# Neighbourhood attention on TensorE: low products with 66 stationary columns, placed between a step's transposes

## The chip, the cores and the metric

The kernel runs on one core of a Trainium2 chip. The metric is the device time of one execution in microseconds (us); of several runs the median is taken. The engines that matter here are TensorE (PE, with its weight loads as PEld), VectorE (DVE), ScalarE (ACT) and GpSimd (POOL). SyncE (SP) issues most of the DMA transfers. A matrix product on PE has a stationary operand, loaded first (here up to 128 columns, each giving one row of the output), and a moving operand that is streamed through it (here 128 to 512 columns).

## The reference

The reference is an encoder of two layers over 1024 tokens of width 1024. Layer 0 mixes tokens with mixer A, layer 1 with mixer B, and behind each mixer comes a gated embedding; everything is float32. The change touches mixer A alone. Tokens lie on a grid 64 wide, and each query attends to a window of 8 rows by 16 columns around it, with a bias by head and offset. Cut to what matters:

```python
proj = h @ w_in
q, k, v, gate = jnp.split(proj, 4, axis=-1)        # 16 heads of 64
...
def row_block(args):
    ...
    sc = jnp.einsum('bhqd,bhqnd->bhqn', qb, kg) * scale
    sc = sc + bb[None]
    pr = jax.nn.softmax(sc, axis=-1)
    return jnp.einsum('bhqn,bhqnd->bhqd', pr, vg)
...
return (o * jax.nn.silu(gate)) @ w_out
```

## The kernel before, in words

**Precision.** Products run on PE in fp32r, a rounded float32. To keep float32's accuracy each operand is split into a high part and a low part (what the rounding left), and three of the four products are added up: high by high, high by low, low by high. In names `h` and `l` at the end are the two parts: `HTh`/`HTl` the normalised activations, `wh`/`wl` a weight tile, `PTh`/`PTl` the attention weights transposed.

**Tiling of mixer A.** The 1024 tokens are 8 tiles of 128. A tile's window reaches into its own tile and its two neighbours, so an inner tile has three pieces of 128 keys and an outer one has two. The main loop runs over 16 heads h and 8 tiles j; a pair (h, j) is a step. It occupies the stretch from 64 to 520 us of the profiled execution. Each step issues a piece of a pipeline:

- `f_S` (line 741): scores of the step three ahead, two products `s<-KA,QS` and `s<-KB,QS`; DVE then adds the bias table (line 760).
- `f_E` (765): ACT's exponential of the step two ahead, in `sp`.
- `f_T` (770): this step's weights are transposed on PE, two transposes `t<-ident,sp` (776). Two tiles are enough for three pieces, since the two outer pieces of an inner tile use complementary rows and share one tile. ACT copies them to `PTh` (781), DVE takes the rest to `PTl` (782), and for inner tiles POOL parts the shared piece into two by masks (`apart`, 786), first of `PTh`, then of `PTl`. These two land in the key tiles j−1 and j+1.
- `f_AV` (793): the products with v of the step three behind, for the key tile kb: `o<-PTh,V`, then `o<-PTl,V` (the "high" and the "low" product). `V` has 128 stationary columns: 64 of v's high part and 64 of its low part, so an output `o` has 128 rows, and `head_end` adds the upper 64 to the lower ones later. A key tile serves the queries of up to three tiles, so the moving operand is 256 or 384 columns wide; for kb 3 and 4 it is split in two (256 and 128 columns), as the queries 0 to 3 and 4 to 7 have outputs of their own. The products of kb need the masks of tiles kb−1 and kb+1, so the last `PTh` that they wait for is that of tile kb+1, transposed two steps ahead of them. After kb 4 and kb 7 half a head is complete and `head_end` (482) is called.

**What sets the order.** Everything is written out by hand in program order, one queue per engine. `mix` (366) interleaves a list `att` of the steps' pieces with a list of dense blocks (projections of q, k and the gate for later heads: six products of 512 columns to a block) by costs; after each piece or block a counter ticks. `CA` (31) holds the costs: head, f_T, f_E, f_S, f_AV = 1.0, .5, 1.25, 1.0, .75. What `head_end` leaves for later (`post`) is due so many ticks after it: among it `rows` (496), which transposes the reciprocal row sums on DVE (`r8T`, 498), stores them to DRAM by four DMAs (`rD`, 501) and reads them back, spread over 64 partitions, by two (`rb`, 503). Then comes `fin` (563), POOL's products `Y*G` (574) and `Y*rb` (575). All these DMAs stand in SP's queue, and there the weight loads of `Weights.stage` (`wstage`, 211; two stage buffers) stand too. ACT splits a weight tile to `wh` (228) when it has landed, DVE subtracts for `wl` (233). Every fourth head (3, 7, 11) also computes v for the next four heads behind its products.

Of the kernel before, what the change touches and what calls it, by code (L numbers as in the profile page):

```python
# [21 lines left out]
NT = 8  # L22
# [3 lines left out]
NH = 16  # L26
# [4 lines left out]
CA = (1.0, 0.5, 1.25, 1.0, 0.75)  # L31
# [7 lines left out]
FIN = (4, 4)  # L39
# [10 lines left out]
YS = (11, 11)  # L50
YLOAD_A, YLOAD_B = 0, 118
OPEN3 = 5
ULOAD = 5
TAGS_A = [("th", 512, 2), ("tb", 640, 2), None, ("G", 512, 3)]
TAGS_B = [("th", 512, 2)]
# [105 lines left out]
def trunk(ctx, tc, x, wts, rpb, gains, hgains, mask, sides, rope, gain0, out):  # L161
# [118 lines left out]
    def load_y(l, t):  # L280
        for i, (d, src) in enumerate(zip((HTh, HTl), yD[l])):
            k0 = 4 if i and t >= 4 else 0
            (act if t < 4 else sync).dma_start(d[:, t, k0:7].bitcast(F32), src[t, :, k0:7])
# [34 lines left out]
    def mm(ps, a, b, first, last):  # L318
        pe.matmul(ps, a, b, start=first, stop=last, skip_group_check=True)  # L319
# [333 lines left out]
    def mixer_a():  # L653
        jobs = weight_sums()
        with ExitStack() as es:
# [4 lines left out]
            sb = es.enter_context(tc.tile_pool(name="asb", bufs=2))  # L660
            V = one.tile([128, NT, 4, 128], F32R, name="V")
# [9 lines left out]
            gg, ylive = {}, {}  # L671
            QS, KA, KB, TB, RS, SP, OP, UT = {}, {}, {}, {}, {}, {}, {}, {}
            later = Later()

            def v_items(qd, t, thirds=None):
                keys = [("av", qd, 0), ("av", qd, 1)]

                def evac(ps):
                    v = ps.rearrange("p (h d) -> p h d", h=4)
                    act.activation(V[:, t, :, 0:64], v, AF.Copy)  # L680
                    dve.tensor_tensor(V[:, t, :, 64:128], v, V[:, t, :, 0:64], ALU.subtract)
                return [d[0] for d in proj_N(keys, t, 256, valloc, evac, release=keys if t == NT - 1 else (), thirds=thirds)]
# [39 lines left out]
            def load_u(h):  # L722
                UT[h] = sb.tile([128, 16, 24], F32, name="u", bufs=1)
                sync.dma_start(UT[h], U2[h].rearrange("p (r c) -> p r c", r=16))

            def table(h):
                u = UT.pop(h)
                tb = sb.tile([128, 640], F32, name="tb").rearrange("p (k c) -> p k c", k=5)
                for k, c0 in ((0, 0), (1, 0), (2, 8), (3, 16), (4, 16)):
                    pool.tensor_tensor(tb[:, k].rearrange("p (r c) -> p r c", r=16),  # L730
                                       MK[:, k].rearrange("p (r c) -> p r c", r=16),
                                       u[:, :, c0:c0 + 8], ALU.subtract)
                TB[h] = tb

            def join(h):
                dve.copy_predicated(TB[h][:, 1], SIDE[:, 2].bitcast(mybir.dt.int32), TB[h][:, 3])

            def near(j):
                return max(j - 1, 0), min(j + 1, NT - 1)
# [25 lines left out]
            def f_E(h, j):  # L765
                n = 256
                sp, mn = SP[h, j]
                act.activation(sp[:, :n], sp[:, :n], AF.Exp, bias=mn, scale=-1.0, accum_out=RS[h][:, j:j + 1])

            def f_T(h, j):  # L770
                sp, _ = SP.pop((h, j))
                ps = psT.tile([128, 4, 128], F32, name="t")
                inner = 0 < j < NT - 1
                for i in range(2):
                    c = 1 - i if inner else i
                    pe.transpose(ps[:, i], sp[:, c * 128:(c + 1) * 128], ident)
                k0 = near(j)[0]
                f0 = 3 * j + 1 if inner else k0 * 3 + (j - k0 + 1)
                f1 = 3 * NT + j % 2 if inner else f0 + 2
                sl = slice(f0, f1 + 1, f1 - f0)  # L780
                act.activation(PTh[:, sl], ps[:, :2], AF.Copy)  # L781
                dve.tensor_tensor(PTl[:, sl], ps[:, :2], PTh[:, sl], ALU.subtract)
                if inner:
                    def apart():
                        for pt in (PTh, PTl):
                            pool.tensor_tensor(pt[:, 3 * j - 1:3 * j + 4:4], pt[:, f1:f1 + 1].to_broadcast([128, 2, 128]), SIDE[:, :2],  # L786
                                               ALU.mult)
                    apart()
# [4 lines left out]
            def f_AV(h, kb):  # L793
                if kb == 0:
                    OP[h] = [None, None]
                j0, j1 = near(kb)
                for hf in range(2):
                    a, b = max(j0, 4 * hf), min(j1, 4 * hf + 3)
                    if a > b:
                        continue  # L800
                    first = OP[h][hf] is None
                    if first:
                        OP[h][hf] = psO.tile([128, 512], F32, name="o")
                    o = OP[h][hf][:, (a - 4 * hf) * 128:(b + 1 - 4 * hf) * 128]
                    s0 = kb * 3 + a - kb + 1
                    sl = slice(s0, s0 + b - a + 1)
                    last = kb == (4 if hf == 0 else 7)
                    mm(o, V[:, kb, h % 4], PTh[:, sl], first, False)
                    mm(o, V[:, kb, h % 4], PTl[:, sl], False, last)
                    if last:  # L810
                        fin = head_end(sb, h, hf, RS[h][:, 4 * hf:4 * hf + 4], OP[h][hf], ylive, 0, gg, talloc)
                        if fin:
                            later.add(FIN[0], fin)

            e2 = es.enter_context(ExitStack())
            ini = e2.enter_context(tc.tile_pool(name="ini", bufs=1))
# [64 lines left out]
            part, base, rest = wk[:, 24:25], wk[:, 25:26], wk[:, 26:27]  # L881
# [67 lines left out]
            PTl = ptp.tile([128, NT * 3 + 2, 128], F32R, name="PTl")  # L949
# [16 lines left out]
            steps = [(h, j) for h in range(NH) for j in range(NT)]  # L966

            def av_and_v(h, kb):
                fs = [(lambda: f_AV(h, kb), CA[4])]
                if h % 4 == 3 and h < NH - 1:  # L970
                    fs += [(f, 0.0) for f in v_items(h // 4 + 1, kb)]
                return fs

            for h in range(NH):
                att = []
                for j in range(NT):
                    n = h * NT + j
                    def head(h=h, j=j):
                        later.tick()
                        if j == 1 and h + 1 < NH:  # L980
                            table(h + 1)
                        if j == 5 and h + 1 < NH:
                            join(h + 1)
                        if h >= 1 and j != 1 and jobs:
                            jobs.pop(0)()
                        if j == ULOAD and h + 2 < NH:
                            load_u(h + 2)
                    att.append((head, CA[0]))
                    att.append((lambda h=h, j=j: f_T(h, j), CA[1]))
                    if n + 2 < len(steps):  # L990
                        att.append((lambda n=n: f_E(*steps[n + 2]), CA[2]))
                    if n + 3 < len(steps):
                        att.append((lambda n=n: f_S(*steps[n + 3]), CA[3]))
                    if n >= 3:
                        att += av_and_v(*steps[n - 3])
                    if h == 15 and j >= YLOAD_A:
                        for t in ((j - YLOAD_A,) if j < NT - 1 else range(j - YLOAD_A, NT)):
                            att.append((lambda t=t: load_y(0, t), 0.0))
                    if h == 14 and j == OPEN3:
                        att.append((open3, 0.0))  # L1000
                if h == NH - 1:
                    att += [(lambda k=k: f_AV(NH - 1, k), CA[4]) for k in range(NT - 3, NT)]
                dense = []
                if h < NH - 1:
                    dense += qk_items(h + 1)
                p = h // 2
                if h < 14:
                    dense += gate_items("ag", p, h % 2, dalloc, sb, gg)
                elif h == 14:
                    dense += gate_items("ag", 7, 0, dalloc, sb, gg) + gate_items("ag", 7, 1, dalloc, sb, gg)  # L1010
                else:
                    dense += pp_items(0, dalloc, sb, TAGS_A, lambda: qkp.tile([128, 1024], F32R, name="QS"))
                mix(att, dense, 4 if h == 0 else 0, HOLD if h == NH - 1 else 0)
# [761 lines left out]
    U2 = dram.tile([16, 128, 384], F32, name="U2")  # L1775
    ropeD = dram.tile([2, NT, 128, 2, 64], F32, name="ropeD")
    mixer_a()
    pend = dense_phase(0)
    mixer_b(pend)
# [19 lines left out]
```

## Time and profile before

| | |
|---|---|
| runs | 1516.16, 1518.08 and 1517.87 us, median 1517.87 us |
| profiled execution | span of 1514.0 us from the first to the last instruction |
| mean granted TensorE clock | 0.998 |
| stage of mixer A's steps | 64 to 520 us of the span |
| `t<-ident,sp` in it | 256 transposes |
| `o<-PTl,V` in it | 64 of 384 columns, 64 of 256, 32 of 128 |
| POOL's `apart` in it | 96 × `PTh` (81.0 us), 96 × `PTl` (89.7 us) |

The span is that of one profiled execution; a run's time has some microseconds around it. A group's row gives its busy time and the mean of one; matmuls overlap in the pipeline, so that the mean is longer than the distance from one to the next. A row of a timeline gives the start, the duration, the engine, the line, what is written from what, and the shapes. In brackets stands idle time of the engine just before it, and what ended it.

### The profile page before, as it was taken

The page shows a single profiled execution, that of the slowest core. Times are in us where ns is not written, and L with a number is a line of the kernel's source. Part 1 is how long each engine was busy: PE and PEld are TensorE (multiplying, and loading weights), DVE is VectorE, ACT ScalarE, POOL GpSimd, SP SyncE. Part 2 cuts the span into 40 slices and gives each one's busy share as a digit, 9 for nine tenths or more (in the row PEclk, how much of TensorE's full clock was granted, in tenths as well). Part 3 has the DMA queues.
Part 4 walks back from the last instruction along what each step waited for, and adds up shares of the span by engine and source line. Part 5 has one row for each costly group of instructions (what it writes and reads, how often), then busy time and mean ns, then how long its engine had stood idle before and what let it go on. Part 6 is the DMA issues. An engine that isn't in the chain of part 4 may idle for free.

```text
span 1514.0 us, 24782 instructions
## 1 busy us (share of the span) xinstructions
PE 1483.9 (98%) x8880; PEld 1305.0 (86%) x8880; DVE 1087.9 (72%) x2139; ACT 917.5 (61%) x1865; POOL 450.8 (30%) x605
## 2 busy tenths in 40 slices
PE   8999999999999999999999999999999999999997
PEld 8788988988988787888988999989999988888786
DVE  7566476477467499767887786777877887689856
ACT  6667476477477535443467776666767777744432
POOL 1356376387265200010222132453131300000022
PEclk9999999999999999999999999999999999999999
DMA  8235374274122863262210111111101122763123
GB/s 261 94 110 138 70 175 151 64 160 106 36 88 83 321 249 98 84 192 97 76 51 22 33 40 50 46 33 43 58 27 48 38 77 70 236 233 118 60 91 132
DMA packets 91242, 157.43 MB, mean 104 GB/s; under 512 B 18160, under 2 KB 54256, under 8 KB 90608
## 3 DMA queue, kind: packets, MB, share of 16 engines
q1 hardware_dynamic: 85968, 139.86, 28.2%
q0 software_dynamic: 2560, 8.39, 3.7%
q10 hardware_dynamic: 2592, 7.61, 1.5%
q8 instruction: 70, 1.15, 0.3%
q14 instruction: 52, 0.43, 0.1%
HBM read 125.30 MB, written 50.83 MB: 116 GB/s over the span
## 4 chain that ended last, share of the span: by engine, by line
PE 43%; DVE 6%; ACT 2%; issue 1%; DMA 0%; POOL 0%; ACTq 0%; DVEq 0%; POOLq 0%
PE d L319 19%; PE s L319 8%; PE o L319 8%; PE t L1246 7%; PE t L319 1%; DVE xn L1581 1%; DVE PTl L1249 1%; DVE X L1477 0%; DVE mn L1230 0%; PE t L1200 0%; DVE wl L233 0%; DVE HTl L480 0%; DVE HTl L1423 0%; ACT wh L228 0%; ACT P L1236 0%
## 5 line engine op out<-in xcount | busy, mean ns | idle before, releaser
L319 PE MATMUL d<-wh,HTh 128*128 128x256 f32 (+1 forms) x1000 | 332.9, 335 | 2.7 <-ACT HTh L479 1.7
L319 PE MATMUL d<-wh,HTl 128*128 128x256 f32 (+1 forms) x1000 | 328.9, 331 | 0.3 <-DVE HTl L480 0.3
L319 PE MATMUL d<-wl,HTh 128*128 128x256 f32 (+1 forms) x1000 | 327.9, 330 | 0.2 <-DVE wl L1375 0.2
L1249 DVE TENSOR_TENSOR PTl<-t,PTh 128x512 fp32r<-128x512 f32 x256 | 164.6, 684 | 106.3 <-ACT PTh L1248 106.0
L319 PEld LDWEIGHTS d<-wh,HTh 128*128 128x128 f32 x1000 | 188.5, 189 | 22.7 <-ACT HTh L479 2.0
L319 PEld LDWEIGHTS d<-wl,HTh 128*128 128x128 f32 x1000 | 188.5, 189 | 19.7 <-DVE wl L1375 0.6
L319 PEld LDWEIGHTS d<-wh,HTl 128*128 128x128 f32 x1000 | 188.8, 190 | 18.8 <-DVE HTl L480 0.5
L319 PE MATMUL d<-HTh,wh 128*128 128x512 f32 x504 | 204.7, 406 | 0.0
L319 PE MATMUL d<-HTh,wl 128*128 128x512 f32 x504 | 198.0, 393 | 0.0
L319 PE MATMUL d<-HTl,wh 128*128 128x512 f32 x504 | 197.4, 392 | 0.0
L1236 ACT ACTIVATE P<-s,mn 128x1024 f32<-128x1024 f32 x128 | 142.9, 1116 | 47.3 <-DVE mn L1230 46.4
L1248 ACT ACTIVATE PTh<-t 128x512 fp32r<-128x512 f32 x256 | 139.4, 595 | 46.0 <-PE t L1246 45.5
L1230 DVE TENSOR_REDUCE mn<-s 128x1 f32<-128x1024 f32 x128 | 155.0, 1211 | 9.9 <-PE s L319 9.4
L786 POOL TENSOR_TENSOR PTh<-PTh,SIDE 128x256 fp32r<-128x256 f32 x96 | 81.0, 844 | 197.1 <-ACT PTh L781 197.1
L1246 PE MATMUL t<-ident,P 128*128 128x128 f32 x1024 | 134.8, 273 | 2.6 <-DVE PTl L1249 2.0
L319 PE MATMUL s<-KA,QS 128*128 128x512 f32 (+2 forms) x384 | 134.2, 404 | 2.8 <-DVE mn L760 2.8
L1246 PEld LDWEIGHTS t<-ident,P 128*128 128x128 f32 x1024 | 115.5, 140 | 12.8 <-DVE PTl L1249 6.9
L319 PE MATMUL s<-KB,QS 128*128 128x512 f32 (+2 forms) x384 | 121.4, 370 | 0.0
L319 PE MATMUL o<-PTl,V 128*128 128x256 f32 (+2 forms) x672 | 120.1, 290 | 1.1 <-DVE PTl L1249 0.6
L233 DVE TENSOR_TENSOR wl<-wstage,wh 128x1024 fp32r<-128x1024 f32 x78 | 98.1, 1259 | 31.6 <-ACT wh L228 31.3
L319 PE MATMUL o<-PTh,V 128*128 128x256 f32 (+2 forms) x672 | 118.4, 287 | 2.4 <-POOL PTh L786 1.1
L319 PEld LDWEIGHTS d<-HTh,wl 128*128 128x128 f32 x504 | 94.6, 188 | 21.7
(247 smaller groups left out, 2891.8 us busy)
## 6 DMA issues: line engine op xcount, KB each, us to landing
wstage<-in_wts SPq DMA_DIRECT2D x88, 512.0 KB
pp<-ppD SPq DMA_DIRECT2D x32, 256.0 KB
X<-in_x SPq DMA_DIRECT2D x15, 512.0 KB
rb<-rD SPq DMA_DIRECT2D x56, 128.0 KB
ppD<-th SPq DMA_DIRECT2D x20, 256.0 KB
tD0t<-in_wts SPq DMA_DIRECT2D x16, 256.0 KB
tD1t<-in_wts SPq DMA_DIRECT2D x16, 256.0 KB
xD<-X SPq DMA_DIRECT2D x8, 512.0 KB
```

The source lines that it names most:

```text
L233: eng.tensor_tensor(lo[:, c:c + n], s[:, c:c + n], hi[:, c:c + n], ALU.subtract)
L319: pe.matmul(ps, a, b, start=first, stop=last, skip_group_check=True)
L786: pool.tensor_tensor(pt[:, 3 * j - 1:3 * j + 4:4], pt[:, f1:f1 + 1].to_broadcast([128, 2, 128]), SIDE[:, :2], ALU.mult)
L1230: dve.tensor_reduce(mn, ps, axis=AX.X, op=ALU.min)
L1236: act.activation(p, ps, AF.Exp, bias=mn, scale=-1.0, accum_out=RS[h, hf][:, t:t + 1])
L1246: pe.transpose(ps[:, i], p[:, k * 128:(k + 1) * 128], ident)
L1248: act.activation(PTh[:, ks, c], ps, AF.Copy)
L1249: dve.tensor_tensor(PTl[:, ks, c], ps, PTh[:, ks, c], ALU.subtract)
L1581: dve.scalar_tensor_tensor(xn, X[t], rn[m][:, i:i + 1], g1, op0=ALU.mult, op1=ALU.mult)
```

## The change

The products with v are taken apart. `f_AV` issues the high products only, and puts the low ones into a list `lows`. The low ones then use the first 66 of V's 128 stationary columns and write the first 66 rows of the output: the low part of the weights is no longer multiplied with most of v's low part, a term that the other splits of the kernel leave out too. They are issued in the next `f_T`: the first transpose, a low product, the second transpose, and for kb 3 and 4, which have two, the second low product behind it. `f_AV` moves from the end of a step to its start, behind `head` and ahead of `f_T`; what v's projections issue stays at the end. `head_end` is called with the last low product. For the last three key tiles of head 15, high and low products are issued together as before, with the narrow low ones.

```diff
+NARROW = 66
...
+            lows = []
...
                 inner = 0 < j < NT - 1
+                low = lows.pop(0) if lows else []
                 for i in range(2):
                     c = 1 - i if inner else i
                     pe.transpose(ps[:, i], sp[:, c * 128:(c + 1) * 128], ident)
+                    if low:
+                        low.pop(0)()
+                while low:
+                    low.pop(0)()
...
                 j0, j1 = near(kb)
+                low = []
                 for hf in range(2):
...
                     mm(o, V[:, kb, h % 4], PTh[:, sl], first, False)
-                    mm(o, V[:, kb, h % 4], PTl[:, sl], False, last)
-                    if last:
-                        fin = head_end(sb, h, hf, RS[h][:, 4 * hf:4 * hf + 4], OP[h][hf], ylive, 0, gg, talloc)
-                        if fin:
-                            later.add(FIN[0], fin)
+
+                    def rest(hf=hf, o=o, sl=sl, last=last):
+                        mm(o[:NARROW], V[:, kb, h % 4, :NARROW], PTl[:, sl], False, last)
+                        if last:
+                            fin = head_end(sb, h, hf, RS[h][:, 4 * hf:4 * hf + 4], OP[h][hf], ylive, 0, gg, talloc)
+                            if fin:
+                                later.add(FIN[0], fin)
+                    low.append(rest)
+                lows.append(low)
...
                     att.append((head, CA[0]))
+                    av = av_and_v(*steps[n - 3]) if n >= 3 else []
+                    att += av[:1]
                     att.append((lambda h=h, j=j: f_T(h, j), CA[1]))
...
-                    if n >= 3:
-                        att += av_and_v(*steps[n - 3])
+                    att += av[1:]
...
                 if h == NH - 1:
-                    att += [(lambda k=k: f_AV(NH - 1, k), CA[4]) for k in range(NT - 3, NT)]
+                    def end(k):
+                        f_AV(NH - 1, k)
+                        for f in lows.pop():
+                            f()
+                    att += [(lambda k=k: end(k), CA[4]) for k in range(NT - 3, NT)]
```

Lines behind the first edit move by one to three: `mm` is line 320, the transposes are line 779.

On PE, ahead of the transposes of step (4, 5); `d` are products of a dense block, numbers behind `wh` and `wl` tell weight tiles apart. Before:

```order
L319 MATMUL d<-HTh,wh_1761 128x512
L319 MATMUL d<-HTl,wh_1761 128x512
L319 MATMUL d<-HTh,wl_1762 128x512
L319 MATMUL o<-PTh,V 128x384
L319 MATMUL o<-PTl,V 128x384
L776 MATMUL t<-ident,sp 128x128 x2
L319 MATMUL d<-HTh,wh_1939 128x512
L319 MATMUL d<-HTl,wh_1939 128x512
L319 MATMUL d<-HTh,wl_1940 128x512
```

On PE, the same place in the changed kernel, from the scores of the step ahead to the second transpose of (4, 5):

```order
L320 MATMUL s<-KA,QS 128x256
L320 MATMUL s<-KB,QS 128x256
L320 MATMUL o<-PTh,V 128x384
L320 MATMUL d<-HTh,wh_1935 128x512
L320 MATMUL d<-HTl,wh_1935 128x512
L320 MATMUL d<-HTh,wl_1936 128x512
L320 MATMUL d<-HTh,wh_1935 128x512
L320 MATMUL d<-HTl,wh_1935 128x512
L320 MATMUL d<-HTh,wl_1936 128x512
L779 MATMUL t<-ident,sp 128x128
L320 MATMUL o<-PTl,V 66x384
L779 MATMUL t<-ident,sp 128x128
```

The dense block that stood behind the transposes of this step stands ahead of them, and the low product has come between the two.

On PE, two steps on, where the products of a key tile come in two halves (kb 3), before:

```order
L319 MATMUL d<-HTh,wl_1940 128x512
L319 MATMUL o<-PTh,V 128x256
L319 MATMUL o<-PTl,V 128x256
L319 MATMUL o<-PTh,V 128x128
L319 MATMUL o<-PTl,V 128x128
L776 MATMUL t<-ident,sp 128x128 x2
L319 MATMUL d<-HTh,wh_1939 128x512
```

On PE, the same place in the changed kernel, around the transposes of (4, 6):

```order
L320 MATMUL d<-HTh,wl_1936 128x512
L320 MATMUL o<-PTh,V 128x256
L320 MATMUL o<-PTh,V 128x128
L779 MATMUL t<-ident,sp 128x128
L320 MATMUL o<-PTl,V 66x256
L779 MATMUL t<-ident,sp 128x128
L320 MATMUL o<-PTl,V 66x128
L320 MATMUL d<-HTh,wh_1935 128x512
```

The low products of 66 columns follow one transpose each, and the high products stand side by side ahead of them; they now come one pair of transposes earlier (those of (4, 6) rather than those of (4, 7) stand next behind them).

On SP, in head 4 (heads 8 and 12 are the same), `in_wts` are the weights in DRAM and `u` is a bias table. Before:

```order
L501 DMA rD<-r8T 8x32 x4
L503 DMA rb<-rD 64x512 x2
L211 DMA wstage<-in_wts 128x1024 x2
L501 DMA rD<-r8T 8x32 x4
L503 DMA rb<-rD 64x512 x2
L724 DMA u<-U_90 128x384
L211 DMA wstage<-in_wts 128x1024
```

On SP, the same place in the changed kernel:

```order
L502 DMA rD<-r8T 8x32 x4
L504 DMA rb<-rD 64x512 x2
L502 DMA rD<-r8T 8x32 x4
L504 DMA rb<-rD 64x512 x2
L212 DMA wstage<-in_wts 128x1024 x2
L726 DMA u<-U_90 128x384
L212 DMA wstage<-in_wts 128x1024
```

The two weight loads stand behind the second group of `rD` and `rb`, where they stood ahead of it. On DVE the transpose `r8T` of this group stands ahead of two subtractions for `wl` that were ahead of it. POOL's order is the same as before.

## The prediction

> **What bounds the kernel now.** I read the page first, then the windows over the stage that is edited, the groups by line and tile there, and last the timelines of PE, ACT, POOL, DVE and SP around single steps. T(h,j) is the start of the first transpose of head h, tile j; a "high" product is `o<-PTh,V`, a "low" one `o<-PTl,V`.
>
> ```profile
> span 1514.0 us, 24782 instructions
> PE 1483.9 (98%) x8880; PEld 1305.0 (86%) x8880; DVE 1087.9 (72%) x2139; ACT 917.5 (61%) x1865; POOL 450.8 (30%) x605
> 60.00:520.00 460.00, 456.25 (x2585) 398.94 (x2584) 284.38 (x705) 291.80 (x676) 253.05 (x322) 1.00 0.43 118
> ```
>
> The last line is the windows' row for 60 to 520 us, which covers mixer A's steps: length, then busy time of PE, PEld, DVE, ACT, POOL, the granted clock (1.00), the DMA share, GB/s. TensorE is busy in 456 of 460 us and no other engine in more than 292. So PE's own stream sets the time of the stage, and a change pays or costs in two ways only: what PE spends between the starts of neighbouring products, and waits that the new order brings to PE. Everything outside this stage has the same instructions, so it keeps its 1054 us.
>
> **What is edited on PE.** The transposes and the largest group of low products in the stage (by form: calls, busy us and mean ns, idle before):
>
> ```profile
> L776 PE MATMUL t<-ident,sp 128*128 128x128 f32 x256 | 49.0, 273 | 0.0
> L319 PE MATMUL o<-PTl,V 128*128 128x384 f32 x64 | 21.8, 340 | 0.5 <-DVE mn L760 0.2 <-DVE s L757 0.2
> ```
>
> The means overlap in the pipeline, so they are no prices. Prices come from start to start in PE's timeline, twice within head 4:
>
> ```profile
> 190.57 0.38 PE L776 MATMUL t<-ident,sp 128*128 128x128 f32 x2
> 190.71 0.47 PE L319 MATMUL d<-HTh,wh 128*128 128x512 f32 x1
> 191.02 0.39 PE L319 MATMUL d<-HTl,wh 128*128 128x512 f32 x1
> 191.25 0.40 PE L319 MATMUL d<-HTh,wl 128*128 128x512 f32 x1
> ...
> 198.49 0.22 PE L319 MATMUL o<-PTh,V 128*128 128x128 f32 x1
> 198.54 0.28 PE L319 MATMUL o<-PTl,V 128*128 128x128 f32 x1
> 198.66 0.34 PE L319 MATMUL o<-PTh,V 128*128 128x256 f32 x1
> 198.83 0.28 PE L319 MATMUL o<-PTl,V 128*128 128x256 f32 x1
> 198.95 0.39 PE L319 MATMUL d<-HTh,wh 128*128 128x512 f32 x1
> ```
>
> A 512-wide product takes .23 (191.02 to 191.25), so 256 take .118 and 128 take .059 in proportion. From 190.57 to 191.02 stand two transposes and one 512-wide product: .45, of which .22 are the transposes, where proportion gives .12. From 198.49 to 198.95 stand two products of 128 and two of 256 columns: .46 where proportion gives .354. In both, two short products cost .05 each beyond proportion, and in both each of them is followed by an instruction with 128 stationary columns. I read this as the next load, about .11, being covered by a product of 256 columns or more and only half covered by one of 128. So a short product before a wide load costs an exposure of .051.
>
> **The first term: exposures.** Before, the two transposes of a step stand together and the product behind them loads 128 columns: two exposures. In the changed order a low product of 66 columns stands between them. If its load takes time by its columns (.057), the first transpose covers it, and the low product, when 256 or 384 wide, covers the second transpose's load. One exposure goes in each of 125 steps (the first three have no low product to place). In the two steps per head whose products come in halves of 256 and 128, there are four exposures before (high 128, low 128, two transposes), and two after: 32 more. 157 × .051 = **−8.0 us**. The dense products and the projections of v change their neighbours by an entry or two of the list, not their number or their price; the last three tiles of head 15 keep low beside high.
>
> How long a load of 66 columns takes no row shows: all stationary operands here have 128. Bounds: .11 as the wide one (then a transpose exposes it just the same, and the same count gives a saving of 0) and nothing at all (then no more goes than the 8.0, since .057 is already covered). I take the proportion, .057.
>
> The Trainium skill, "TensorE: Matmul & The Clock Gate", section "LDWEIGHTS (loading the stationary operand)", says that a load takes its columns divided by 1.2 in ns, 107 for 128 and 55 for 66; the trace agrees for 128 with the .11 above, and no run here shows 66 yet. Its section on weight-path perf modes speaks against the change: a faster load is to be had for 128 columns only, so 66 would lose it; but the .11 of the wide load is the plain rate, so there is nothing to lose. By the first rule the term is −8.0 as well, by the second, if it did bite, 0.
>
> **The second term: what PE is made to wait.** The transposed weights travel from PE to ACT (`PTh` copy), to POOL (masks of `PTh`, then of `PTl`), and back to the products of the neighbouring tiles. Three steps' worth of PE work is the slack. The high product moves from the step's end to ahead of its transposes, so this lead shrinks. Summed from the changed order at the prices above, from T(4,5): second high of kb 4 at +4.38, high of kb 5 at +7.97, its low at +8.20; before it was 8.1 and 11.8 for these two highs (198.66 and 202.41 against 190.57). The rows:
>
> ```profile
> 202.07 0.40 PE L319 MATMUL d<-HTh,wl 128*128 128x512 f32 x1
> 202.41 0.45 PE L319 MATMUL o<-PTh,V 128*128 128x384 f32 x1
> 203.09 0.45 PE L319 MATMUL o<-PTl,V 128*128 128x384 f32 x1 [0.23 <-DVE s L757]
> ```
>
> ```profile
> 192.18 1.05 ACT L228 ACTIVATE wh<-wstage 128x1024 fp32r<-128x1024 f32 x1
> ```
>
> ```profile
> 195.40 0.74 POOL L786 TENSOR_TENSOR PTh<-PTh,SIDE 128x256 fp32r<-128x256 f32 x1 [1.46 <-ACT PTh L781]
> ...
> 199.57 1.30 POOL L575 TENSOR_TENSOR Y<-Y,rb 128x512 f32<-128x512 f32 x1 [0.55 <-DMA rb<-rD]
> ...
> 201.35 1.00 POOL L786 TENSOR_TENSOR PTh<-PTh,SIDE 128x256 fp32r<-128x256 f32 x1
> 202.07 0.96 POOL L786 TENSOR_TENSOR PTl<-PTl,SIDE 128x256 fp32r<-128x256 f32 x1
> ```
>
> Kb 4 of head 4 needs the mask that POOL ends at 195.40 + .74 = 196.14, 5.57 after T(4,5): 1.19 later than +4.38. Ahead of ACT's copy for it stands the weight split `wh`, which starts when its DMA lands. SP issues that load here:
>
> ```profile
> 187.82 2.98 SPq L211 DMA_DIRECT2D wstage<-in_wts  x2
> 190.86 1.33 SPq L501 DMA_DIRECT2D rD<-r8T  x4
> 195.57 1.09 SPq L503 DMA_DIRECT2D rb<-rD  x2
> ```
>
> ```profile
> 190.30 0.20 DVE L498 STREAM_TRANSPOSE r8T<-r 128x32 f32<-128x32 f32 x1
> ```
>
> In the new order of heads 4, 8 and 12 these two weight loads stand behind the four stores to `rD` and the two loads of `rb`, and an `rb` load holds SP until `rD` has landed (4.7 from 190.86 to 195.57). What helps: `r8T` comes two list entries earlier and ahead of two weight subtractions on DVE, and T(4,5) itself comes some 1.3 later, because a dense block of six 512-wide products (6 × .23) moves ahead of it. From the load's issue to the end of the mask it takes 196.14 − 187.82 = 8.32, so PE waits only where the load is issued later than 3.94 ahead of T(4,5); it is 2.75 ahead now. Bounds: .4 (the load moves a little ahead of now) and 4.0 (`rb` blocks SP for as long as it does now). I take 1.0, near the 1.19 that today's row gives.
>
> From then on POOL sets the pace: the next mask ends at 202.35, 6.21 after 196.14, of which .55 was idle for `rb`, which now comes earlier: 5.66. PE is there in 3.59: 2.1 more. Its low part ends at 203.03, .68 later, where PE comes .23 later: .45. Head 4: 1.0 + 2.1 + .45 = 3.55, less the .6 that PE waits there already (.34 for .23, .68 for .18): **+2.95**. Head 8 is alike, but PE waits more there now:
>
> ```profile
> 320.64 0.40 PE L319 MATMUL d<-HTh,wl 128*128 128x512 f32 x1
> 322.18 0.44 PE L319 MATMUL o<-PTh,V 128*128 128x384 f32 x1 [1.14 <-POOL PTh L786]
> 322.87 0.45 PE L319 MATMUL o<-PTl,V 128*128 128x384 f32 x1 [0.24 <-DVE mn L760]
> ```
>
> 1.54 for .23 and .69 for .18 are 1.8: 3.55 − 1.8 = **+1.75**. Head 12 waits nowhere now, and its masks are:
>
> ```profile
> 428.93 0.38 PE L776 MATMUL t<-ident,sp 128*128 128x128 f32 x2
> ```
>
> ```profile
> 433.75 0.74 POOL L786 TENSOR_TENSOR PTh<-PTh,SIDE 128x256 fp32r<-128x256 f32 x1 [3.02 <-ACT PTh L781]
> ...
> 438.71 0.74 POOL L786 TENSOR_TENSOR PTh<-PTh,SIDE 128x256 fp32r<-128x256 f32 x1
> 439.40 1.20 POOL L786 TENSOR_TENSOR PTl<-PTl,SIDE 128x256 fp32r<-128x256 f32 x1
> ```
>
> The first ends 5.56 after its T, so again 1.0; the second 439.45, 4.96 after the first: 1.4 over 3.59; its low part 1.15 later: .9 over .23. **+3.3**. Heads 2, 6 and 10 do the same POOL work a step later without the weights:
>
> ```profile
> 123.68 0.38 PE L776 MATMUL t<-ident,sp 128*128 128x128 f32 x2
> ```
>
> ```profile
> 129.33 1.19 POOL L786 TENSOR_TENSOR PTl<-PTl,SIDE 128x256 fp32r<-128x256 f32 x1
> ```
>
> The low mask ends 6.84 after T(2,6), and the low product of kb 5 is due at +6.0: .8 each, **+2.5** for three heads. In the other steps the masks end earlier than the shortened lead, so they cost nothing; that cover is thin (a few tenths in tiles 4 of the even heads).
>
> **Sum.** −8.0 + 2.95 + 1.75 + 3.3 + 2.5 = +2.5 us on a span of 1514.0: 1516.5. The profiled execution has 1514.0, the median of the runs 1517.87, so 3.9 lie around the span: 1520.4. That is within .2% (3.0 us, from 1514.8 to 1520.9, about what a measurement can tell from no change).
>
> **The rivals.**
> - *The waits mostly do not come.* For it: POOL is busy in 253 of 460 us and ACT in 292, so a chain that is late at one step can be early at the next, and `r8T` far enough ahead clears SP before the weights are wanted. Against: the masks' ends are rows, and POOL's work between two masks is the same. Half of the waits in heads 4, 8, 12 and none in the others: −8.0 + 4.0 = −4.0, **1513.9**; none at all 1509.9.
> - *Slower: the weight loads behind `rD`'s landing.* For it: 4.7 between `rD` and `rb` in the row above. If SP holds the weights as long, kb 4 waits 4.0, not 1.0, at three heads: +9.0, **1529.4**. It decides once the loads are issued less than 2.94 ahead of T(h,5) (1.0 of wait); each us later than that is a us more.
> - *The narrow load is no shorter.* The change then does not do what it is written for: saving 0, waits as in the sum, +10.5: **1528.4**. Against it: nothing but proportion.
>
> **Chances.** Forecast .54 (1514 to 1525: faster .04, same .36, slower .14), waits stay away .30 (1510 to 1514.8: faster), weights late .11 (slower), narrow load as long as the wide .05 (slower). Together faster .34, same .36, slower .30. The range from 1511.0 to 1527.5 leaves out a tenth on each side: the no-wait end of the first rival, and most of the other two.
>
> **What the next profile would show.** Right: in PE's timeline the second transpose starts about .23 after the first, with a low product of 384 between them (.059 + .174), and where PE doesn't wait a head takes .5 less. Right: rows of high products at tile 4 and 5 of heads 4, 8, 12 wait for POOL `PTh`, and low ones of kb 5 in heads 2, 6, 10 for `PTl`. SP's row `wstage` of head 4 stands behind `rb`. Wrong would be waits of PE at other steps, a distance of .11 from the first transpose to the low product, or a sum of waits under 8 us.

## The result, and the profile after

The changed kernel takes 1532.62 us (median of 4 runs, 1530.66 to 1535.38), the one before 1517.01 us beside it (4 runs, 1515.46 to 1518.08). The ratio is 1.0105, with a 95% interval from 1.0091 to 1.0120. It is slower by some 16 us, outside the range of 1511.0 to 1527.5, and the forecast of 1520.4 was wrong.

From the page of the changed kernel (span, share of the engines), and its windows' row for 60 to 520 us, with columns as before:

```profile
span 1528.7 us, 24780 instructions
PE 1489.2 (97%) x8880; PEld 1304.5 (85%) x8880; DVE 1087.4 (71%) x2139; ACT 919.3 (60%) x1865; POOL 452.7 (30%) x605
60.00:520.00 460.00, 447.88 (x2514) 387.49 (x2512) 276.70 (x692) 284.88 (x653) 249.17 (x314) 0.99 0.39 105
```

The span is 14.7 us longer. In the same 460 us PE starts 71 products fewer (2514 against 2585), it is idle 8.4 us longer, and the granted clock is no longer 1.00. The groups by form, 64 to 530 us, show where PE idles (the last field: idle before, and what ended it). First one row of the kernel before, then three of the changed kernel:

```profile
L319 PE MATMUL o<-PTh,V 128*128 128x256 f32 x64 | 18.8, 294 | 0.0
```

```profile
L320 PE MATMUL o<-PTl,V 128*66 128x384 f32 x62 | 25.9, 418 | 2.8 <-POOL PTl L793 2.5
...
L320 PE MATMUL o<-PTh,V 128*128 128x384 f32 x62 | 21.5, 347 | 1.3 <-POOL PTh L793 1.3
L320 PE MATMUL o<-PTh,V 128*128 128x256 f32 x61 | 18.3, 300 | 7.5 <-POOL PTh L793 7.5
```

The high products of 256 columns, with no idle time ahead of them before, now wait 7.5 us for POOL's masks, nearly all of it at kb 4. The starts of the transposes in both timelines give the time from T(h,0) to T(h+1,0):

| head | before | after | what the forecast had there |
|---|---|---|---|
| 1 | 23.69 | 23.61 | −.5 by the first term |
| 3, 7, 11 (here falls the low product of kb 5 of heads 2, 6, 10) | 38.11 | 38.88, 38.88, 38.79 | +.8 − .5 |
| 4 | 32.36 | 36.88 | +3.55 − .5 with the row below |
| 5 (waits of head 4 before) | 24.41 | 23.94 | |
| 8 | 32.36 | 39.01 | +3.55 − .5 with the row below |
| 9 (waits of head 8 before) | 25.62 | 23.94 | |
| 12 and 13 | 56.10 | 58.84 | +3.3 − 1.0 |

So two things differ from the forecast at once: the saving of .5 per head is not there (head 1 has .08), and the waits of heads 4 and 8 are longer. From the first transposes to the last the stage takes 466.1 us, before 451.7: 14.4 more. What else differs between the two spans lies outside the stage: it starts 1.2 later (its start lies between 64.9 and 68.7 us in the executions profiled here, whatever the kernel), and what follows it is 1.0 shorter.

### The profile page after: what moved, and what is told of

Same layout as the page of the kernel before. It is cut to its first block, busy times and chain, and to the rows that moved or that the text cites. A ratio compares the mean times of both kernels' runs of the same rounds, so it can differ in the third digit from the quotient of the medians.

```text
span 1528.7 us, 24780 instructions
## 1 busy us (share of the span) xinstructions
PE 1489.2 (97%) x8880; PEld 1304.5 (85%) x8880; DVE 1087.4 (71%) x2139; ACT 919.3 (60%) x1865; POOL 452.7 (30%) x605
## 4 chain that ended last, share of the span: by engine, by line
PE 43%; DVE 7%; issue 2%; ACT 2%; POOL 0%; ACTq 0%; DVEq 0%; POOLq 0%
PE d L320 18%; PE s L320 8%; PE o L320 8%; PE t L1263 7%; PE t L320 1%; DVE xn L1598 1%; DVE PTl L1266 1%; DVE wl L234 0%; DVE mn L1247 0%; DVE X L1494 0%; PE t L1217 0%; DVE HTl L481 0%; DVE HTl L1440 0%; PE t L479 0%; ACT wh L229 0%
## 5 line engine op out<-in xcount | busy, mean ns | idle before, releaser
L320 PE MATMUL o<-PTl,V 128*128 128x256 f32 (+3 forms) x672 | 129.2, 307 | 3.5 <-POOL PTl L793 2.5
L789 DVE TENSOR_TENSOR PTl<-t,PTh 128x256 fp32r<-128x256 f32 x128 | 53.9, 421 | 103.0 <-ACT PTh L788 102.5
```

## Where the saving went: the first look

PE's timeline of the changed kernel at step (1, 0), the first transpose to the second product behind the second one:

```profile
84.14 0.27 PE L779 MATMUL t<-ident,sp 128*128 128x128 f32 x1
84.17 0.42 PE L320 MATMUL o<-PTl,V 128*66 128x384 f32 x1
84.43 0.28 PE L779 MATMUL t<-ident,sp 128*128 128x128 f32 x1
84.46 0.48 PE L320 MATMUL d<-HTh,wh 128*128 128x512 f32 x1
84.78 0.40 PE L320 MATMUL d<-HTl,wh 128*128 128x512 f32 x1
```

A start may stand too early by what the pipeline still holds, so read over both: from 84.14 to 84.43 a transpose and a low product of 384 take .29, not .059 + .174 = .23. From there to 84.78 a transpose and a product of 512 take .35, not .29. Each transpose costs .11, also the one with a narrow load behind it. Two readings fit. **A**: a load of 66 columns takes as long as one of 128 (the rival of the narrow load). **B**: the load is short, and a transpose costs .11 by itself, so it never was an exposure.

## Where the waits come from: the first look

Head 4 of the changed kernel; PE around kb 4, whose high product has halves of 128 and 256 columns:

```profile
198.78 0.22 PE L320 MATMUL o<-PTh,V 128*128 128x128 f32 x1
201.31 0.41 PE L320 MATMUL o<-PTh,V 128*128 128x256 f32 x1 [2.31 <-POOL PTh L793]
201.54 0.61 PE L320 MATMUL d<-HTh,wh 128*128 128x512 f32 x1
201.94 0.63 PE L320 MATMUL d<-HTl,wh 128*128 128x512 f32 x1
202.37 0.63 PE L320 MATMUL d<-HTh,wl 128*128 128x512 f32 x1
```

The links ahead of this wait, in order of time. SP's timeline:

```profile
188.25 1.28 SPq L502 DMA_DIRECT2D rD<-r8T  x4
191.98 1.09 SPq L504 DMA_DIRECT2D rb<-rD  x2
193.17 1.01 SPq L212 DMA_DIRECT2D wstage<-in_wts  x2
```

ACT's, and then POOL's:

```profile
197.30 1.06 ACT L229 ACTIVATE wh<-wstage 128x1024 fp32r<-128x1024 f32 x1 [3.34 <-DMA wstage<-in_wts]
```

```profile
200.52 0.73 POOL L793 TENSOR_TENSOR PTh<-PTh,SIDE 128x256 fp32r<-128x256 f32 x1 [4.45 <-ACT PTh L788]
```

T(4,5) is at 194.38. SP stands 3.7 us from `rD` to `rb`, issues the weights 1.2 ahead of T(4,5) (2.75 before), ACT waits 3.34 for them, and the mask is ready 6.9 after T(4,5), where PE came 4.5 after it. Behind the wait the products of 512 columns take .43, not .23, for some three us. The windows from 201.3 on and of the following stretch give the granted clock in the column behind POOL:

```profile
201.30:204.40 3.10, 3.09 (x10) 2.43 (x11) 2.68 (x8) 2.01 (x6) 3.02 (x3) 0.54 0.97 296
204.40:207.00 2.60, 2.40 (x12) 1.79 (x10) 1.12 (x2) 2.50 (x6) 2.60 (x4) 0.89 0.22 71
```

So behind this wait PE runs at about half its clock for a while. At head 8 the same is worse: 4.45 of idle time end at 326.95, and ACT's `wh` starts 6.1 after the weights' issue at 316.83 (4.1 in head 4). ACT's row there, and then the windows' row behind the wait:

```profile
322.95 1.06 ACT L229 ACTIVATE wh<-wstage 128x1024 fp32r<-128x1024 f32 x1 [5.50 <-DMA wstage<-in_wts]
```

```profile
326.90:331.30 4.40, 4.35 (x14) 3.66 (x15) 2.73 (x8) 3.11 (x8) 4.32 (x4) 0.51 0.70 214
```

## The experiments

Each kernel ran beside the one before on the same chip; times are medians, the ratio is to the kernel before with its 95% interval.

**1. The narrow product alone, in the old order.**

```diff
-                    mm(o, V[:, kb, h % 4], PTl[:, sl], False, last)
+                    mm(o[:66], V[:, kb, h % 4, :66], PTl[:, sl], False, last)
```

> The kernel before in its old order, only the low products take 66 stationary columns and write 66 rows of the output. It tells two readings of the missing saving apart at the 32 places where a low product of 128 moving columns follows a high one of 128 (kb 3 and 4 of each head). Reading A, a load of 66 columns takes as long as one of 128: high 128, low 128, high 256, low 256 still take .46 us from start to start, time as before (1517). Reading B, the narrow load is short (about .06) and it is the transpose that costs .11 by itself, whatever is loaded behind it: the four take .41, and 32 x .05 = 1.6 us go (1515.4).

1515.97 us (12 runs) against 1517.68 (23 runs), ratio .9993 [.9984, 1.0003]. The time alone decides nothing; the timeline does. The four products of kb 4 in head 4:

```profile
198.94 0.22 PE L319 MATMUL o<-PTh,V 128*128 128x128 f32 x1
199.00 0.22 PE L319 MATMUL o<-PTl,V 128*66 128x128 f32 x1
199.06 0.33 PE L319 MATMUL o<-PTh,V 128*128 128x256 f32 x1
199.24 0.28 PE L319 MATMUL o<-PTl,V 128*66 128x256 f32 x1
199.35 0.40 PE L319 MATMUL d<-HTh,wh 128*128 128x512 f32 x1
```

From 198.94 to 199.35 they take .41; before it was .46. Head 1 takes 23.59, not 23.69: two exposures of .05 per head are gone. The narrow load is short, and reading A falls.

**2. The move alone, with all 128 columns.**

```diff
-NARROW = 66
+NARROW = 128
```

> The changed kernel with all 128 stationary columns in the low products: the move alone. Both readings give the same time as the changed kernel, 1532 (+-1), and .29 us from the first to the second transpose with a low product of 384 between them. If the narrow load is worth what the prediction gave it, .05 at each of about 157 places, this kernel takes 8 us more, 1540, and .34 us.

1534.22 us (4 runs), ratio 1.0110 [1.0095, 1.0124], beside 1.0105 with 66 columns: between the transposes the narrow operand is worth nothing that this can tell, and not 8 us. From the first transpose to the second it is .29 again. Both readings had it so.

**3. SP's old order back.**

```diff
-DO = (2, 3)
+DO = (4, 3)
```

> The changed kernel with head_end's first post due two entries later in layer 0 (DO 4, not 2), which puts the weight loads of heads 4, 8 and 12 ahead of the second group of rD and rb on SP again, as before. Theory: what waits beyond the forecast is the weights late behind rD's landing. Then the waits at kb 4 fall from 2.4, 4.6 and .8 to about 1.2 each, the products of .43 us behind the two long ones (3.2 us) are .23 again, and waits at kb 5 of 2.5 each take part of it back: about 1529. Rival, the shortened lead alone makes the waits: 1532, with the same rows. Other rival, POOL is ahead after all: under 1525.

1527.55 us (4 runs), ratio 1.0070 [1.0054, 1.0085]: near the 1529 of the theory. But the rows are not those expected. Kb 4 does not wait at all, and kb 5 waits 4.2 and 4.6 over its price in heads 4 and 8, not 2.5 (1.0 in head 12). The profiled execution is the longest of the four, 1531.15 us. POOL's timeline in head 4, and then PE's:

```profile
204.15 1.81 POOL L576 TENSOR_TENSOR Y<-Y,rb 128x512 f32<-128x512 f32 x1 [1.92 <-DMA rb<-rD]
```

```profile
207.50 0.44 PE L320 MATMUL o<-PTh,V 128*128 128x384 f32 x1 [4.05 <-POOL PTh L793]
```

With the weights ahead, `rb` lands late, POOL stands in `Y*rb`, and the next mask behind it is late. The two orders on SP pass the same wait from one link to another.

**4. The leads of before, with the low products between transposes.** The high product goes back to the step's end, the low ones wait for the next step's `f_T` (heads 3, 7, 11: at once).

```diff
...
+                    if h % 4 == 3 and h < NH - 1:
+                        flush()
...
-                    av = av_and_v(*steps[n - 3]) if n >= 3 else []
-                    att += av[:1]
...
-                    att += av[1:]
+                    if n >= 3:
+                        att += av_and_v(*steps[n - 3])
```

> The high products at their old place at the step's end, the low ones of 66 columns between the transposes of the step behind (for heads 3, 7 and 11 at once, as v is overwritten there). Leads are as before or longer. Theory: all waits of the changed kernel come from the lead, so they go, and the interleaving by itself saves nothing: 1517, as before, +-1.5. Rival, the interleaving saves the 8 us that were forecast and only waits hide it: 1509.

1515.80 us (12 runs), ratio .9987 [.9978, .9997]: the waits at kb 4 are gone, at kb 5 no more is left than before, and there is no saving of 8. On SP the weights of head 4 stand ahead of `rD` again (187.12 and 190.15), so this kernel takes back the short lead and the new order on SP at once. The group that waited 7.5 us has no wait left:

```profile
L320 PE MATMUL o<-PTh,V 128*128 128x384 f32 x64 | 21.9, 341 | 0.9 <-POOL PTh L793 0.9
L320 PE MATMUL o<-PTh,V 128*128 128x256 f32 x64 | 18.8, 294 | 0.0
```

**5. Old order on SP, and POOL's Y work a step later.**

```diff
-DO = (2, 3)
+DO = (4, 3)
...
-FIN = (4, 4)
+FIN = (5, 4)
```

> Like x3_posts_later (head_end's posts two entries later, so the weights stand ahead of rD and rb on SP), and POOL's Y*G and Y*rb one step later (FIN 5, not 4), behind the mask that kb 5 waits for. Theory: with the weights early, what PE waits for at kb 5 in heads 4, 8 and 12 of x3 (4.2, 4.6 and 1.0 us, and some 3.5 us of half-rate products behind the two long ones) is POOL standing in Y*rb for rb. So these go, kb 4 stays without a wait, and the time comes to 1516 (+-2.5), about that of the kernel before. Rival: the Y work only delays the next mask as much, and the waits go on one tile later: over 1523.

1523.33 us (6 runs), ratio 1.0035 [1.0023, 1.0046]: 4 less than experiment 3 and 7 more than expected, at the edge of the rival. The waits at kb 5 are gone, and new ones stand *earlier*, at kb 3, in each of the three heads, 1.4 at the high and .45 at the low half of 128. Head 4 on PE, and then on POOL:

```profile
198.86 0.33 PE L320 MATMUL o<-PTh,V 128*128 128x128 f32 x1 [1.42 <-POOL PTh L793]
```

```profile
194.46 1.30 POOL L575 TENSOR_TENSOR Y<-Y,G 128x512 f32<-128x512 f32 x1
195.84 1.29 POOL L576 TENSOR_TENSOR Y<-Y,rb 128x512 f32<-128x512 f32 x1
...
197.64 1.17 POOL L793 TENSOR_TENSOR PTh<-PTh,SIDE 128x256 fp32r<-128x256 f32 x1
```

Each pair of heads has two such pieces of Y work, one for each half of the tokens. The first one of heads 2 and 3, a step later too (it started at 185.35 in experiment 3), now stands ahead of the mask that kb 3 of head 4 needs.

**6. The changed kernel with only the Y work a step later.**

```diff
-FIN = (4, 4)
+FIN = (5, 4)
```

> The changed kernel with only POOL's Y work a step later (FIN 5), SP's order as changed. Theory: the waits at kb 4 are the weights behind rb and stay (2.4, 4.6 and .8 us, with 3.2 us at half rate), those at kb 5 (.7, .3 and 2.0) go, and those of .9 at kb 5 in heads 2, 6 and 10 too: 1526.5 (+-2). Rival, POOL's Y work is behind all of it: 1517.

1518.49 us (10 runs), ratio 1.0005 [.9995, 1.0015]: not to be told from the kernel before. The theory expected 1526.5; the rival was right on the time. Head 4 on SP:

```profile
186.19 1.28 SPq L502 DMA_DIRECT2D rD<-r8T  x4
188.39 1.10 SPq L504 DMA_DIRECT2D rb<-rD  x2
189.59 1.01 SPq L212 DMA_DIRECT2D wstage<-in_wts  x2
```

`rb` follows `rD` after 2.2, not 3.7, so the weights go out 2.7 ahead of T(4,5) (192.31). What fits is that a DMA of POOL, which the changed kernel issues behind the Y work at 187.51, just ahead of `rD` at 188.25, goes out at 182.50 here. That it is this DMA was not tried alone, but the changed kernel's own heads agree: in head 8 such a DMA goes out .7 ahead of `rD`, and `rb` follows after 3.9; in head 12 none goes out in the 6 us ahead of `rD`, and `rb` follows after 2.2. ACT's rows, in heads 4 and 8:

```profile
195.38 1.06 ACT L229 ACTIVATE wh<-wstage 128x1024 fp32r<-128x1024 f32 x1 [3.49 <-DMA wstage<-in_wts]
...
314.39 1.06 ACT L229 ACTIVATE wh<-wstage 128x1024 fp32r<-128x1024 f32 x1 [2.25 <-DMA wstage<-in_wts]
```

The earlier issue pays in head 8: ACT has the weights 1.8 after T(8,5), where it was 5.1 in the changed kernel, and kb 4 waits no more. In head 4 it does not: there the weights take 5.8 from their issue to ACT, not 4.1, and are used 3.1 after T(4,5), not 2.9. Kb 4 waits .8 there, not 2.3, because the mask, with less ahead of it on ACT, ends .4 earlier after T(4,5), and because PE comes later, as it has waited .6 at kb 3 behind the Y work. Why the same loads take 4.1 in one place and 5.8 in another stays open.

**7. The weight loads on ACT's queue.** Only for heads 3, 4, 7, 8, 11 and 12.

```diff
+            self.via = sync
...
-                sync.dma_start(s, wts[UNIT[key]])
+                self.via.dma_start(s, wts[UNIT[key]])
...
+                WQ.via = act if h in (3, 4, 7, 8, 11, 12) else sync
```

> The changed kernel with the weight loads of heads 3, 4, 7, 8, 11 and 12 issued by ACT's DMA queue, not SP's, so that they no longer stand behind rb, which holds SP until rD has landed. Theory: at kb 4 of heads 4 and 8 PE waits for weights that SP issues late; issued by ACT they start earlier by the 3.7 us between rD and rb, the waits of 2.4 and 4.6 us fall to at most 1.2 and no products run at half rate behind them (-8 us), while POOL's Y work then makes PE wait up to 2.5 at kb 5 in each (+4): 1528 (+-2). Rival: the transfers themselves are slow there, as the DMA engines are full, and SP's queue has no part in it: 1532, with the same rows.

1522.49 us (10 runs) against 1516.75 (13 runs), ratio 1.0035 [1.0022, 1.0048]: 10 less than the changed kernel, where 4 were expected. Head 4 in ACT's timeline, and then in PE's:

```profile
189.95 0.34 ACTq L213 DMA_DIRECT2D wstage<-in_wts  x1
191.14 0.34 ACTq L213 DMA_DIRECT2D wstage<-in_wts  x1
```

```profile
203.14 0.45 PE L321 MATMUL o<-PTh,V 128*128 128x384 f32 x1 [1.14 <-POOL PTh L794]
```

With T(4,5) at 193.68 the first load goes out 3.7 ahead, kb 4 waits no more, and kb 5 waits 1.1 at the high product for POOL, less than the up to 2.5 expected. In head 8 it is the same with 1.5 at kb 5. So in these two heads it is SP's queue, held by `rb`, that makes the weights late. In head 12, where SP was held least (2.2 us), the waits stay as they were in the changed kernel: the weights go out 3.7 ahead of T(12,5) there, not 2.7, but ACT has them 5.2 after their issue, not 4.0. For this head the rival fits, the transfers themselves.

**8. Transposes in fp32r.** ACT writes the exponentials to a tile in fp32r, and the identity is fp32r; the attention weights are rounded there, so that their low parts are zero.

```diff
...
-                    pe.transpose(ps[:, i], sp[:, c * 128:(c + 1) * 128], ident)
+                    pe.transpose(ps[:, i], sp[:, c * 128:(c + 1) * 128], identr)
...
```

> The changed kernel with the step's two transposes in fp32r, not fp32: ACT writes the exponentials to a tile of their own in fp32r (they are rounded there, so that the low parts PTl come out as zero), and the moving identity is fp32r too. Reading B, a transpose in fp32 costs .11 by itself: from the first transpose over a low product of 384 to the second it takes .235, not .29. Rival, the transpose exposes its load or something else that the type doesn't touch: .29 as before. Time: about 1525 by B, with the waits, 1532 by the rival.

One run: 1529.9 us. (The scores keep two buffers, not four, to make room.) PE's timeline at a step of head 1:

```profile
86.94 0.22 PE L783 MATMUL t<-identr,sr 128*128 128x128 f32 x1
87.00 0.34 PE L322 MATMUL o<-PTl,V 128*66 128x384 f32 x1
87.17 0.22 PE L783 MATMUL t<-identr,sr 128*128 128x128 f32 x1
87.23 0.39 PE L322 MATMUL s<-KA,QS 128*128 128x384 f32 x1
87.46 0.33 PE L322 MATMUL s<-KB,QS 128*128 128x384 f32 x1
```

From the first to the second transpose it takes .23, not .29. In fp32r the transpose costs its .059, and the narrow load behind it is hidden: reading B holds. The second transpose has a load of 128 columns behind it (`KA`): from 87.17 to 87.46 it and a product of 384 take .29, .05 more than the .23 of proportion. So a transpose in fp32r pays the exposure that the prediction had read, and a narrow neighbour takes it away. The time of this one run is hardly lower, though: PE waits 4.79 at kb 4 of head 4, where it was 2.31, as the weights, issued 1.1 ahead of T(4,5), take 6.4 to ACT, not 4.1.

**9. What the readings give in the old order.** Narrow low products, and where there are halves: wide high, short high, short low, wide low, so that no short product has a wide load behind it.

```diff
+                todo = []
-                for hf in range(2):
+                for hf in (0, 1) if kb != 4 else (1, 0):
...
+                    def rest(hf=hf, o=o, sl=sl, last=last):
+                        mm(o[:66], V[:, kb, h % 4, :66], PTl[:, sl], False, last)
...
+                    todo.append(rest)
+                for f in todo[::-1]:
+                    f()
```

> The kernel before in its old order of steps with low products of 66 columns, and where kb has two halves the order is high 256, high 128, low 128, low 256. By reading B (short products pay .05 when the load behind them is wide) none of the four is followed by a wide load while short: all four exposures per head go, twice as many as in x1: 64 x .05 = 3.2 us, 1514.3 against 1517.5. If the load of 66 hides no better behind 128 columns than x1 showed by chance: 1517.

1514.00 us (9 runs) against 1517.22 (22 runs): the 3.2 us expected, ratio .9980 [.9966, .9993]. In its trace head 1 takes 23.50, .19 less than before, which is the four exposures. This version is faster than both kernels.

## Why the prediction was wrong, point by point

**"One exposure goes in each of 125 steps": this step failed.** The prediction read the .05 that a transpose costs beyond proportion as the load behind it, because the products of 128 columns showed the same .05. The same size has two causes. For products in fp32r the reading holds: a narrow load behind them takes the .05 away (experiment 1), at 64 places it is worth 3.2 us (experiment 9). A transpose in fp32 takes .11 by its type and not by its neighbour (experiment 8). The term of −8.0 came out as some −.1 per head, −1.3 in all (head 1's .08 × 16). The rows before the change could not tell the two apart, as every transpose there has a wide load behind it.

**The rival "the narrow load is no shorter"** gave nearly the right consequence, a saving of 0, from the wrong cause. That its 1528.4 is only 4 off is luck, as its waits are those of the forecast.

**The waits of heads 2, 6 and 10** were right: +.8 each forecast, .88, .88 and .79 measured as what the low product of kb 5 has over its price.

**"I take 1.0" for kb 4 of heads 4, 8 and 12: mis-sized**, inside the bounds for two heads and outside for one. Over the price it is 2.4, 4.6 and .8, 7.8 where 3.0 were forecast. In heads 4 and 8 the mechanism was the one named, the weights behind `rb` on SP; experiment 7 shows it by taking them out of that queue. The loads went out 1.2 ahead of T(4,5), and by the prediction's own 3.94 that makes 2.7: the choice of 1.0 for the place of the load was the error. The upper bound of 4.0 came from head 4, and head 8's weights took 6.1 to be used.

**At kb 5** 2.1 + .45 were forecast for heads 4 and 8, and they have .7 and .3: PE, late from kb 4 and slowed behind it, gives POOL the time. Head 12 came as forecast (1.2 + .8 for 1.4 + .9).

**The clock was missing.** No term stood for what a wait does to the products behind it. Behind the two long waits PE ran at about half its clock. By the windows' rows what it lost is (1 − .54) × 3.1 + (1 − .89) × 2.6 = 1.7 us in head 4 and (1 − .51) × 4.4 = 2.2 in head 8, 3.9 in all.

**The sum again.** Waits 7.8 + 2.8 (heads 2, 6, 10: the three above and .2 at a high product of head 10) + 3.1 (kb 5) + .3 (head 0, kb 3) = 14.0, half clock 3.9, less the 2.4 of waits before and the 1.3 of narrow loads: 14.2 of the 14.4 by which the stage is longer. The waits of kb 5 fell short of the forecast by more than 4 us, which hid part of what was too small elsewhere.

**What bounds the kernel** was right: PE's stream and the waits brought to it. The rival "slower" named the right place with 1529.4, at a chance of .11; that its number is near is luck in part, as it has the saving of 8.0 in it and no clock. That the lead decides is shown by experiments 3 and 4 together: with SP's old order and the short lead the time is still 10 us over the kernel before, with the old lead it is not. Restoring one link only hands the wait on: experiments 3 and 5 move it to `rb` and to POOL's Y work. Experiment 6 shows that a shift of that work by one step is enough to lose most of the waits with the short lead.

## What to carry to other kernels

Before a cost beyond proportion is put down to the neighbour, look for the same instruction with another neighbour, or of another type; if the trace has none, the saving has 0 as an equal end. A product moved ahead of its old place shortens the lead of all that feeds it, DMA queues included: sum each chain to the new due time, and where two links are near it, expect that mending one shows the other. A wait of PE of 1.5 us or more may have slower products behind it, here 1.7 and 2.2 us for the two long ones; it is to be priced with them.

## What the runs showed of the hardware that was not expected

A transpose of 128 columns in fp32 takes .11 us of PE's stream, in fp32r .06. A load of 66 stationary columns is hidden behind a product of 128 columns (.059), one of 128 columns is not. By the rule in the Trainium skill, "TensorE: Matmul & The Clock Gate", section "LDWEIGHTS (loading the stationary operand)", the former is estimated at 55 ns, and experiment 1 agrees with that as far as it shows.

After 2.31 us without work PE ran at a granted clock of .54 for 3.1 us; after 2.10 us, at 503.85 in the kernel before, it went on at .23 for a product of 512 (504.19 to 504.42). In experiment 4 that same place had 2.6 over its price, and a clock of .50 behind it. The row of the wait before, and the windows' row of experiment 4:

```profile
503.85 0.50 PE L319 MATMUL d<-wh,KA 128*128 128x512 f32 x1 [2.10 <-ACT th L617]
```

```profile
503.00:505.00 2.00, 2.00 (x8) 1.87 (x7) 0.55 (x3) 1.62 (x5) 0.81 (x2) 0.50 0.93 278
```

The length of a wait does not decide it alone, for in experiment 7 the 1.49 of head 8 was enough (products of 512 take .43 behind it), and in experiment 5 the same two waits, 1.42 and .45, stand in heads 4, 8 and 12, but only behind those of head 4 the clock falls. The windows' rows of heads 4 and 8:

```profile
200.70:204.00 3.30, 3.30 (x11) 2.82 (x10) 3.30 (x1) 0.00 (x0) 2.94 (x4) 0.50 0.96 288
321.40:325.40 4.00, 3.98 (x22) 3.42 (x23) 3.97 (x2) 0.22 (x1) 3.68 (x5) 1.00 0.90 213
```

The Trainium skill, "TensorE: Matmul & The Clock Gate", section "What's actually happening", has a window of some 3.4 us by which the clock is set, running freely. The length of the slow stretches agrees, and so does experiment 5, where the place of a wait and not its length made the difference. The advice of the same page of the Trainium skill, section "Why this matters for your kernels", to keep idle gaps under about 3 us is too generous for these rows.
